# Batched fp32 matmul, A times B transposed: stores of batches 4 and 5 in parts in place of batch 11's

## The chip, the cores and the metric

The kernel runs on one core of a Trainium2 chip. The metric is the device time of one execution in microseconds, as the median of several runs. A profile of one execution goes with it; its span runs from the first to the last instruction.

## What is computed

For 16 batches the product of a 512 x 512 matrix with the transpose of another, in fp32:

```python
batch, m, k, n = 16, 512, 512, 512
np.matmul(a, b.transpose(0, 2, 1)).astype(np.float32)
```

Both inputs are 16.8 MB, and so is the output: 33.56 MB are read from HBM and 16.78 MB written.

## The kernel before

The 16 batches are worked off in 8 pairs `u`; a pair is batches `2u` (`e` = 0) and `2u+1` (`e` = 1).

**Loads.** A load brings the `a` or the `b` of one pair: 2 MB, on 128 partitions with 16 KB each. Load `n` is `a` of pair `n/2` for even `n`, `b` for odd `n`; there are 16. Seven buffers `ld` take them in turn (slot `n % 7`). Load 1 is issued by SP, all others by ACT: loads 0 to 6 at the start, then two at a time after the `ta` copies of a pair (lines 192 to 194).

**GpSimd** waits for each load in order and then adds one to `s_go` (lines 107, 108). DVE takes one of `s_go` before it reads a load.

**DVE** casts a load to bf16 in halves of K: the first half into `ha` or `hb`, the second into `wa` or `wb`, from where it is copied to `ha` or `hb` later.

**TensorE** transposes the bf16 blocks into PSUM (`tp`). ACT copies the transposed `a` into `ta` (line 181), DVE the transposed `b` into `tb` (line 168). Then come 32 matmuls of a pair (line 242), which write four PSUM banks `ps` for each batch.

**ACT** evicts `ps` into `ob` (line 201), four copies a batch. There are seven output buffers `ob`, so before it evicts batch `n` it waits until the store of batch `n - 7` has landed (line 198): `landed(n)` is semaphore `s_st[n % 7]` at a multiple of 16. ACT's instructions are in one fixed order for all pairs: eight `ta` copies, loads, four evictions of the first batch, four of the second. After the second batch's first and last eviction it adds one to `s_out`, so `s_out` at `n + 1` says that batch `n` is out of PSUM.

**Stores.** SP waits at the start for a second use of load slot 0 (line 120, load 7), then for `s_out` at `n + 1`, and stores batch `n`: 1 MB, each partition four consecutive rows of 2 KB, 8 KB in one run. The last batch is stored in two parts, the fourth row of each partition at the end (line 263).

**Batch 11 is stored otherwise** (`X = 11`). Its middle rows 1 and 2 of each partition go out as one DMA. Rows 0 and 3 go out in parts: SP stores partitions 32 to 95 in one DMA, then partitions 0 to 15 as four DMAs of four partitions each, then 16 to 19. GpSimd, after its loop over the loads, waits for `s_out` at 12 and issues four groups of three DMAs: a read of five short rows of `a` into `turn`, which nothing uses, then three partitions of 20 to 31, then eight of 96 to 127. SP's parts count on `s_x`, GpSimd's on `s_y`, and ACT waits for both at the end (lines 257, 258), together with the landings of the last seven stores.

Of the kernel before, what the change touches and what calls it, by code (L numbers as in the profile page):

```python
# [10 lines left out]
def kernel(  # L11
# [6 lines left out]
    nc = tc.nc  # L18
    P = 128
    batch, M, K = a.shape  # L20
    _, N, _ = b.shape
    J = M // P
# [3 lines left out]
    pairs = batch // 2  # L26
    f32 = mybir.dt.float32
    bf16 = mybir.dt.bfloat16
    NL = 7
    NO = 7  # L30
    X = 11

    def sbuf(name, shape, dtype):
        return ctx.enter_context(nc.sbuf_tensor(name, shape, dtype))

    def sem(name):
        return tc.alloc_semaphore(name)

    with tc.tile_critical(no_gpsimd_drain=True):  # L41
# [8 lines left out]
        ob = sbuf("ob", [P, NO, J, N], f32)  # L50
# [5 lines left out]
        s_ld = [sem(f"s_ld{i}") for i in range(NL)]  # L56
        s_st = [sem(f"s_st{i}") for i in range(NO)]

        s_go = sem("s_go")
# [11 lines left out]
        s_out = sem("s_out")  # L71
        s_x = sem("s_x")
        s_y = sem("s_y")
# [5 lines left out]
            out=ident[:], in_=ident[:], compare_op=mybir.AluOpType.not_equal, fill=1.0,  # L79
# [6 lines left out]
        def load(n, engine):  # L86
            u, slot = n // 2, n % NL
            src = (a if n % 2 == 0 else b)[2 * u:2 * u + 2].rearrange(
                "e (p j) k -> (e p) j k", j=2 * J
            )  # L90
            engine.dma_start(ld[:, slot], src).then_inc(s_ld[slot], 16)

        def landed(n):
            return s_st[n % NO], 16 * (n // NO + 1)

        def store(n, lo=0, hi=J, step=1, part=slice(0, P), engine=nc.sync):
            rows = slice(lo, hi, step)
            return engine.dma_start(  # L98
                out[n].rearrange("(p j) n -> p j n", j=J)[part, rows], ob[part, n % NO, rows]
            )  # L100

        load(0, nc.scalar)
# [1 line left out]
        for n in range(2, NL):  # L104
            load(n, nc.scalar)

        for n in range(2 * pairs):
            nc.gpsimd.wait_ge(s_ld[n % NL], 16 * (n // NL + 1)).then_inc(s_go, 1)  # L108

        nc.gpsimd.wait_ge(s_out, X + 1)
        for i in range(4):
            nc.gpsimd.dma_start(  # L114
                turn[:5, i], a[0, :5, :64].rearrange("p (x k) -> p x k", x=2)[:, :, :16]
            ).then_inc(s_y, 16)
            for part in (slice(20 + i, 32, 4), slice(96 + i, P, 4)):
                store(X, step=J - 1, part=part, engine=nc.gpsimd).then_inc(s_y, 16)

        nc.sync.wait_ge(s_ld[0], 32)  # L120
        for n in range(batch):
            nc.sync.wait_ge(s_out, n + 1)
            if n != X:
                store(n, hi=J if n < batch - 1 else J - 1).then_inc(landed(n)[0], 16)
                continue


            store(n, lo=1, hi=J - 1).then_inc(landed(n)[0], 16)
            store(n, step=J - 1, part=slice(32, 96)).then_inc(s_x, 16)
            for i in range(4):  # L130
                store(n, step=J - 1, part=slice(i, 16, 4)).then_inc(s_x, 16)
            store(n, step=J - 1, part=slice(16, 20)).then_inc(s_x, 16)

        def taker(engine):
            return lambda s, n: engine.wait_ge(s, n).then_inc(s, -n)  # L135
# [9 lines left out]
        with nc.Fori(0, pairs, engines=[dve]) as u:  # L145
            for x, (h, w, s_c, s_w) in enumerate(
# [4 lines left out]
                if x == 0:  # L151
# [4 lines left out]
                    out=h[:, J:, :], in_=src[:, J:, :HK]  # L156
                ).then_inc(s_c, 1)
                nc.vector.tensor_copy(out=w[:], in_=src[:, :, HK:]).then_inc(s_w, 1)  # L158
            for ko in range(KO):
# [5 lines left out]
                if ko == 1:  # L165
# [3 lines left out]
                    out=tb[:, ko, :],  # L169
# [7 lines left out]
        for u in range(pairs):  # L177
            for ko in range(KO):
                nc.scalar.wait_ge(s_ta, KO * u + ko + 1)
                for e in range(2):  # L180
                    c = nc.scalar.copy(  # L181
                        out=ta[:, ko, e * J * P:(e + 1) * J * P].rearrange(
                            "k (j p h) -> k j p h", j=J, h=2
                        ),
                        in_=tp[:, ko % 2, :, e * HP:(e + 1) * HP].rearrange(
                            "k (h j) p -> k j p h", h=2
                        ),
                    )
                c.then_inc(s_ea, 1)


            for n in (2 * u + NL, 2 * u + NL + 1):
                if n < 2 * pairs:
                    load(n, nc.scalar)
            for e in range(2):
                n = 2 * u + e
                if n >= NO:
                    nc.scalar.wait_ge(*landed(n - NO))
                for j in range(J):
                    nc.scalar.wait_ge(s_mm, J * n + j + 1)  # L200
                    c = nc.scalar.copy(  # L201
                        out=ob[:, n % NO, j, :].rearrange("m (p j) -> m p j", j=2 * J),
                        in_=ps[:, j, :].rearrange("m (j p) -> m p j", j=2 * J),
                    )
                    if e == 0:
                        c.then_inc(s_pv, 1)
                    elif j in (0, J - 1):
                        c.then_inc(s_out, 1)
# [45 lines left out]


    with tc.tile_critical(sync_engine=act, no_gpsimd_drain=True):
        nc.scalar.wait_ge(s_x, 16 * 6)
        nc.scalar.wait_ge(s_y, 16 * 12)
        for n in range(batch - NO, batch):
            nc.scalar.wait_ge(*landed(n))  # L260
    waits = nc.cur_bb.bb.instructions[-1]
# [38 lines left out]
```

## Time and profile before

| | before |
|---|---|
| median of 3 runs | 124.81 us (124.76 to 124.86) |
| profiled execution | 125.12 us |
| its span | 123.3 us |
| moved by DMA | 50.35 MB, mean 408 GB/s over the span |
| busy: PE, DVE, ACT, GpSimd | 73%, 55%, 55%, 7% of the span |
| store queue q1, load queue q10, GpSimd's q0 | 36.2%, 60.5%, 0.5% of 16 DMA engines' span |
| longest wait of ACT behind a store | 4.4 us, of 5.9 us in two |

The busy row of the page cuts the span into 40 slices of 3.1 us and gives each engine's busy share in tenths. The DMA row is the mean over the core's 16 DMA engines. "q10" holds the loads that ACT issues, "q1" what SP issues: load 1 and the stores. "q0" holds what GpSimd issues. A packet is one contiguous piece that one DMA engine moves. At the end of each DMA every engine that took part writes the semaphore, which the trace records as a packet of 4 bytes (a completion packet). In a timeline, the square brackets behind a group give the idle time before it and what ended it.

### The profile page before, as it was taken

The numbers are of one execution on the slowest core, as the hardware profiler recorded it, in microseconds if no ns is written. First come the engines' busy times: TensorE is split into PE (matmuls) and PEld (weight loads), VectorE is DVE, ScalarE is ACT, GpSimd is POOL, SyncE is SP. The second block draws the span as 40 slices with busy tenths as digits, with TensorE's granted clock in tenths as the row PEclk, the third lists the DMA queues.
The fourth block names the chain that finished last, engine by engine and source line by source line (L and its number), as shares of the span: only waits on it lengthen the run. The fifth ranks groups of instructions, "written<-read, shape, count | busy, mean of one in ns | idle before, by whom it ended". The sixth has DMA issues, their size and how long they took to land. (4 is left out here: it accounts for less than half of the span.)

```text
span 123.3 us, 2255 instructions
## 1 busy us (share of the span) xinstructions
PE 90.2 (73%) x768; PEld 54.8 (44%) x768; DVE 67.9 (55%) x96; ACT 67.9 (55%) x130; POOL 8.5 (7%) x18
## 2 busy tenths in 40 slices
PE   0000089999999899989998999999799917996000
PEld 0000078447744764574477347645654506542000
DVE  0000598982896589388918974872977059400000
ACT  0400064567855966696589468765866069656000
POOL 2000000000000000000000000000000039910000
PEclk9999999999999999999999999999999999999965
DMA  4999999999999999999999999999999999999991
GB/s 112 404 425 425 441 431 431 431 431 441 425 436 425 425 361 415 444 423 425 431 433 425 431 423 425 436 444 428 423 423 441 412 423 423 432 397 432 425 407 72
DMA packets 5341, 50.35 MB, mean 408 GB/s; under 512 B 904, under 2 KB 904, under 8 KB 1500
## 3 DMA queue, kind: packets, MB, share of 16 engines
q10 hardware_dynamic: 2160, 31.46, 60.5%
q1 hardware_dynamic: 2796, 18.70, 36.2%
q0 software_dynamic: 384, 0.18, 0.5%
q14 instruction: 1, 0.01, 0.0%
HBM read 33.56 MB, written 16.78 MB: 408 GB/s over the span
## 5 line engine op out<-in xcount | busy, mean ns | idle before, releaser
L242 PE MATMUL ps<-tb,ta 128*128 128x512 bf16 x256 | 57.8, 379 | 0.4
L201 ACT COPY ob<-ps 128x512 f32<-128x512 f32 x64 | 34.2, 591 | 27.8 <-PE ps L242 21.9
L181 ACT COPY ta<-tp 128x512 bf16<-128x512 bf16 x64 | 33.0, 612 | 13.7 <-PE tp L223 13.2
L242 PEld LDWEIGHTS ps<-tb,ta 128*128 128x128 bf16 x256 | 24.1, 98 | 30.6 <-issue 4.0
L223 PE MATMUL tp<-ident,ha 128*128 128x128 bf16 x256 | 18.6, 224 | 18.7 <-PEq L135 18.2
L223 PEld LDWEIGHTS tp<-ident,ha 128*128 128x128 bf16 x256 | 15.8, 100 | 22.3 <-issue 20.5
L168 DVE COPY tb<-tp 128x1024 bf16<-128x1024 bf16 x32 | 21.2, 685 | 3.6 <-DVEq L135 3.6
L223 PE MATMUL tp<-ident,hb 128*128 128x128 bf16 x256 | 17.6, 223 | 3.5 <-PEq L135 3.3
L223 PEld LDWEIGHTS tp<-ident,hb 128*128 128x128 bf16 x256 | 15.4, 100 | 4.7 <-issue 4.4
L154 DVE CAST ha<-ld 128x1024 bf16 x8 | 5.5, 690 | 14.6 <-POOLq L108 13.8
L163 DVE COPY ha<-wa 128x2048 bf16<-128x2048 bf16 x8 | 5.5, 691 | 12.7 <-DVEq L135 12.7
L154 DVE CAST hb<-ld 128x1024 bf16 x8 | 5.5, 689 | 7.9 <-DVEq L135 7.9
L158 DVE CAST wa<-ld 128x2048 bf16 x8 | 9.8, 1220 | 0.0
L158 DVE CAST wb<-ld 128x2048 bf16 x8 | 9.8, 1220 | 0.0
L114 POOL DMA_DIRECT2D turn<-in_a_dram x4 | 2.7, 663 | 98.9 <-ACT ob L201 98.9
L155 DVE CAST ha<-ld 128x1024 bf16 x8 | 5.5, 687 | 0.0
L155 DVE CAST hb<-ld 128x1024 bf16 x8 | 5.5, 686 | 0.0
L167 DVE COPY hb<-wb 128x2048 bf16<-128x2048 bf16 x8 | 5.5, 684 | 0.0
L98 POOL DMA_DIRECT2D out_dram<-ob x8 | 5.2, 651 | 0.0
L176 ACT ACT_TABLE_LOAD x1 | 1.3, 1283 | 4.1 <-issue 4.1
L78 POOL TENSOR_SCALAR_AFFINE_SELECT ident<-ident 128x128 bf16<-128x128 bf16 x1 | 0.3, 288 | 0.2 <-POOL ident L76 0.2
L76 POOL MEMSET ident<- 128x128 bf16 x1 | 0.2, 205 | 0.5 <-SPq L41 0.5
(5 smaller groups left out, 0.6 us busy)
## 6 DMA issues: line engine op xcount, KB each, us to landing
ld<-in_a_dram ACTq DMA_DIRECT2D x8, 2048.0 KB, 29.1
ld<-in_b_dram ACTq DMA_DIRECT2D x7, 2048.0 KB, 26.8
out_dram<-ob SPq DMA_DIRECT2D x14, 1024.0 KB, 29.0
ld<-in_b_dram SPq DMA_DIRECT2D x1, 2048.0 KB, 12.5
out_dram<-ob SPq DMA_DIRECT2D x1, 768.0 KB, 8.0
out_dram<-ob SPq DMA_DIRECT2D x1, 512.0 KB, 24.5
out_dram<-ob SPq DMA_DIRECT2D x2, 256.0 KB, 7.9
out_dram<-ob POOLq DMA_DIRECT2D x4, 32.0 KB, 6.0
```

Of the source, the lines that this page charges most:

```text
L98: return engine.dma_start(out[n].rearrange("(p j) n -> p j n", j=J)[part, rows], ob[part, n % NO, rows])
L114: nc.gpsimd.dma_start(turn[:5, i], a[0, :5, :64].rearrange("p (x k) -> p x k", x=2)[:, :, :16]).then_inc(s_y, 16)
L154: nc.vector.tensor_copy(out=h[:, :J, :], in_=src[:, :J, :HK])
L155: nc.vector.tensor_copy(out=h[:, J:, :], in_=src[:, J:, :HK]).then_inc(s_c, 1)
L158: nc.vector.tensor_copy(out=w[:], in_=src[:, :, HK:]).then_inc(s_w, 1)
L163: nc.vector.tensor_copy(out=ha[:], in_=wa[:]).then_inc(s_ca, 1)
L167: nc.vector.tensor_copy(out=hb[:], in_=wb[:]).then_inc(s_cb, 1)
L168: nc.vector.tensor_copy(out=tb[:, ko, :], in_=tp[:, 2 + ko % 2].rearrange("k j p -> k (j p)"),).then_inc(s_eb, 1)
L181: c = nc.scalar.copy(out=ta[:, ko, e * J * P:(e + 1) * J * P].rearrange("k (j p h) -> k j p h", j=J, h=2), in_=tp[:, ko % 2, :, e * HP:(e ...
L201: c = nc.scalar.copy(out=ob[:, n % NO, j, :].rearrange("m (p j) -> m p j", j=2 * J), in_=ps[:, j, :].rearrange("m (j p) -> m p j", j=2 * J),)
L223: t = nc.tensor.transpose(tp[:, 2 * x + g, j, :], h[:, j, g * P:(g + 1) * P], ident[:])
L242: t = nc.tensor.matmul(ps[:, j, :], ta[:, ko, (e * J + j) * P:(e * J + j + 1) * P], tb[:, ko, :].rearrange("k (j p) -> k j p", j=2 * J)[:, ...
```

## The change

The treatment in parts goes from batch 11, rows 0 and 3, to batches 4 and 5, rows 0 and 1 (`X = 4`, `H = 2`):

- Batches 4 and 5: SP stores rows 2 and 3 of each partition at the usual place, one DMA a batch, in runs of 4 KB. Directly after batch 5's, SP issues six DMAs, each over both batches: partitions 32 to 95, then five of four partitions each (0, 5, 10, 15; 1, 6, 11, 16; and so on to 4, 9, 14, 19).
- GpSimd's groups of three DMAs cover the same partitions as before, for both batches at once, in runs of 4 KB. They stand inside its loop over the loads: two groups after load 9, two after load 10, each time after a wait for `s_out` at 6.
- ACT's waits for `s_x` and `s_y` move from the end of the program to the place before batch 11's eviction (batch 11 reuses the buffer of batch 4, slot 4).
- Batch 11 is stored whole, like the others.

```diff
-    X = 11
+    X = 4
+    H = J // 2
@@
-        def store(n, lo=0, hi=J, step=1, part=slice(0, P), engine=nc.sync):
-            rows = slice(lo, hi, step)
+        def store(n, lo=0, hi=J):
+            return nc.sync.dma_start(
+                out[n].rearrange("(p j) n -> p j n", j=J)[:, lo:hi], ob[:, n % NO, lo:hi]
+            )
+
+        def store_two(part, engine):
+
             return engine.dma_start(
-                out[n].rearrange("(p j) n -> p j n", j=J)[part, rows], ob[part, n % NO, rows]
+                out[X:X + 2].rearrange("e (p j) n -> p e j n", j=J)[part, :, :H],
+                ob[part, X % NO:X % NO + 2, :H],
             )
@@
-        for n in range(2 * pairs):
-            nc.gpsimd.wait_ge(s_ld[n % NL], 16 * (n // NL + 1)).then_inc(s_go, 1)
-
-
-
-        nc.gpsimd.wait_ge(s_out, X + 1)
-        for i in range(4):
+        def spare(i):
             nc.gpsimd.dma_start(
                 turn[:5, i], a[0, :5, :64].rearrange("p (x k) -> p x k", x=2)[:, :, :16]
             ).then_inc(s_y, 16)
             for part in (slice(20 + i, 32, 4), slice(96 + i, P, 4)):
-                store(X, step=J - 1, part=part, engine=nc.gpsimd).then_inc(s_y, 16)
+                store_two(part, nc.gpsimd).then_inc(s_y, 16)
+
+        for n in range(2 * pairs):
+            nc.gpsimd.wait_ge(s_ld[n % NL], 16 * (n // NL + 1)).then_inc(s_go, 1)
+            if n in (X + 5, X + 6):
+                nc.gpsimd.wait_ge(s_out, X + 2)
+                for i in range(2):
+                    spare(2 * (n - X - 5) + i)
@@
-            if n != X:
-                store(n, hi=J if n < batch - 1 else J - 1).then_inc(landed(n)[0], 16)
-                continue
-
-
-            store(n, lo=1, hi=J - 1).then_inc(landed(n)[0], 16)
-            store(n, step=J - 1, part=slice(32, 96)).then_inc(s_x, 16)
-            for i in range(4):
-                store(n, step=J - 1, part=slice(i, 16, 4)).then_inc(s_x, 16)
-            store(n, step=J - 1, part=slice(16, 20)).then_inc(s_x, 16)
+            store(n, H if n in (X, X + 1) else 0, J if n < batch - 1 else J - 1).then_inc(
+                landed(n)[0], 16
+            )
+            if n == X + 1:
+
+
+                for part in (slice(32, 96), *(slice(i, i + 16, 5) for i in range(5))):
+                    store_two(part, nc.sync).then_inc(s_x, 16)
@@
                 if n >= NO:
                     nc.scalar.wait_ge(*landed(n - NO))
+                if n == X + NO:
+                    nc.scalar.wait_ge(s_x, 16 * 6)
+                    nc.scalar.wait_ge(s_y, 16 * 12)
@@
     with tc.tile_critical(sync_engine=act, no_gpsimd_drain=True):
-        nc.scalar.wait_ge(s_x, 16 * 6)
-        nc.scalar.wait_ge(s_y, 16 * 12)
         for n in range(batch - NO, batch):
             nc.scalar.wait_ge(*landed(n))
```

## The prediction

> **What bounds the kernel now.** I read the page first, for which resource is never idle. The engines' rows have gaps everywhere; the DMA row has none.
>
> ```profile
> PE   0000089999999899989998999999799917996000
> DMA  4999999999999999999999999999999999999991
> ```
>
> Then the table of stretches for the end, to see whether the transfers are still full once the last compute is over (columns: stretch, its length, PE, PEld, DVE, ACT, POOL, clock, DMA share, GB/s).
>
> ```profile
> 112.00:114.00 2.00, 0.83 (x4) 0.20 (x2) 0.00 (x0) 1.07 (x2) 0.00 (x0) 1.00 1.02 420
> ...
> 116.00:118.00 2.00, 0.00 (x0) 0.00 (x0) 0.00 (x0) 0.00 (x0) 0.00 (x0) 1.00 1.04 441
> 118.00:120.00 2.00, 0.00 (x0) 0.00 (x0) 0.00 (x0) 0.00 (x0) 0.00 (x0) 0.53 0.97 405
> ```
>
> Compute ends at 113.5 us and the DMA engines run full for eight more: 50.35 MB at full rate set the end. The chain of waits, which shows only PE and ACT and ends at 113.5, would mislead. The compute has slack, but little: the last two DMAs are issued at 113.5 and 114.3, and at 113.5 the store queue holds about 4.4 us of data ahead of them (the packet records show batch 15's packets from 117.95). Anything that delays ACT's last eviction by more than that, less about 1.5 us from issue to data, starves the DMA.
>
> Next, how the two big queues share the engines (page of the queues for 46 to 76 us; packets, MB, share of 16 engines).
>
> ```profile
> q10 hardware_dynamic: 586, 8.55, 67.0%
> q1 hardware_dynamic: 575, 4.21, 33.2%
> ```
>
> q10 is the loads (16 KB packets), q1 the stores (8 KB). 8.55 MB are 522 packets, 4.21 MB are 514: one for one, not byte for byte. From the shares (16 engines x 30 us = 480 engine-us), 0.670 x 480 / 522 = 0.616 us for a load packet, 0.332 x 480 / 514 = 0.310 us for a store packet. The packet records give the same: 611, 309, 159 and 84 ns for 16, 8, 4 and 2 KB, the next starting some 4 ns before the end; a pair takes 0.914 us, a store (8 packets an engine) 7.3 us. So the last completion packets of stores 3 to 6 are at 76.77, 84.19, 91.74 and 99.15 us, and the last load lands at 99.42.
>
> Last, ACT's timeline, where those landings come back to compute, through the seven output buffers:
>
> ```profile
> 84.91 2.05 ACT L201 COPY ob<-ps 128x512 f32<-128x512 f32 x4 [1.50 <-DMA out_dram<-ob]
> ...
> 99.84 2.05 ACT L201 COPY ob<-ps 128x512 f32<-128x512 f32 x4 [4.42 <-DMA out_dram<-ob]
> ```
>
> Batch 11 waits for store 4, batch 13 for store 6, each going on 0.7 us after the landing. These are the only stalls behind stores, and the change edits the first.
>
> **What the Trainium skill says.** "DMA: Bandwidth & Descriptors", section "Queues, rings and completion order": each DMA engine goes round its queues packet by packet. The 522 to 514 agrees. Same page, "Why a DMA increments its semaphore by 16 and not by 1": a DMA uses the largest number of engines up to 16 that divides the outer dimension, from SP the lowest-numbered. A four-partition DMA then runs on engines 0 to 3; the trace doesn't name engines, but q1's count of packets (2796) is right for 64 partitions on 16 engines and five such DMAs on four. "TensorE: Matmul & The Clock Gate", Part 1: an idle PE falls to half clock, and some 3.4 us of work bring it back. Here the clock was half at 118.1, 5.2 us after the last matmul, and full at 19.1, 3.8 us after the first; the cold start shows in PE's timeline:
>
> ```profile
> 15.36 1.87 PE L223 MATMUL tp<-ident,ha 128*128 128x128 bf16 x16 [15.36 <-PEq L135]
> ...
> 28.68 1.06 PE L223 MATMUL tp<-ident,ha 128*128 128x128 bf16 x16
> ```
>
> **The change, part by part.**
>
> Bytes. Engine 4 was spared 4 partitions x 2 rows of 2 KB: 8 x 0.080 = 0.64 us. Now it is 4 partitions x 2 batches of 4 KB: 8 x 0.155 = 1.24 us. Engines 0 to 3 carry two extra packets, 0.31 us for 0.16. By the last store's completion packets, one engine ends at 121.72, the next at 121.15, the rest between 120.5 and 121.1. If the last is engine 4, up to 0.57 us can be won; if not, nothing, or 0.15 lost on engines 0 to 3. Taken: -0.3 us, and only if the transfers still set the end.
>
> GpSimd. The twelve DMAs now stand inside the loop that passes each landed load to DVE through s_go: six after load 9, six after load 10. The new wait for s_out at 6 costs nothing: the value is there at 52.5, load 9 lands at 55.5. Behind them are s_go of loads 10 and 11, for which DVE waits. The four groups took 2.7, 1.76, 1.68 and 1.70 us. From 55.5 the first six end at about 60.0, before load 10 lands (62.8); the next six run from 62.8 to some 66.3, before load 11 (70.2). Hidden; with no cover they would delay a cast by up to 4.5 us.
>
> SP. Store 4 and store 5 become halves of 8 packets of 4 KB an engine. Then come, ahead of store 6, the 64-partition DMA (4 partitions x 2 batches, 8 packets) and five DMAs on engines 0 to 3 (10 packets). SP issues them at about 53 us, with 9 us to the next issue; the small ones cost it 0.6 to 0.75 us each, as at 87 to 90 us, so this is free. In q1, engines 0 to 3 now hold 34 packets of 4 KB where 16 of 8 KB stood, the others 24. This is the core of it: as the queues take turns by packet, each of these waits for one 16 KB load packet as long as loads remain. A turn moves half as much store data.
>
> ACT. The waits for s_x and s_y leave the end, where they cost nothing, and stand before batch 11's eviction. Before, it waited for store 4. Now it waits for everything down to the last small DMA behind stores 4 and 5. Behind the waiting instruction are batch 11's evictions, all `ta` copies of pairs 6 and 7 and all later evictions; behind those PE, SP's stores from batch 10 on, and the end.
>
> When does s_x arrive? Store 3's completion packets come from 75.15 to 76.77, median 75.7; these loads and stores are unchanged on engines 0 to 3. At that point some 25 load packets an engine are left (loads 13, 14, 15, and one of load 12). A turn is now 0.608 + 0.155 = 0.763 us. 25 turns: 19.1 us. The loads are then done, and the last 9 small-DMA packets follow alone: 9 x 0.155 = 1.4. So 20.5 us after 75.7 to 76.8: 96.2 to 97.3. On engines 5 to 15, GpSimd's 8 packets of 4 KB cost 1.3 us earlier, and 24 turns take 18.3: 94.7 to 96.4. I take 96.7. The loads end about 4 us earlier than before, which is where the stores' turns go; this doesn't help, as ACT stands still.
>
> From there, each duration from the timeline: wake-up 0.7, batch 11's evictions 2.05: 99.5 (before: 86.96). Pair 6 at the undisturbed pace (29.5, 41.0, 52.45: 11.5 us a pair) plus a cold PE, which has been idle since about 88: 32 transposes of the second half took 2.1 us warm, at half clock some 3.6; partly beside ACT's copies, so +1.1 (bounds 0 and 2): 112.1. Pair 7: 11.5, so ACT ends at 123.6, not 113.5. The stall of 4.42 us before batch 13 vanishes inside this: store 6 lands by about 99.
>
> And the DMA: stores 6 to 9 fill it from 96.7 to about 106, batches 10 and 11 to 111, 12 and 13 (out of ACT at 110 and 112) to about 116. Batch 14 leaves ACT only at 121.4. So it idles some 5 us. After 123.6: about 1.5 us from issue to data (first load: 1.0; SP's first: 1.9), 8 x 0.230 for 6 KB packets and 8 x 0.080 for the last row, together 2.5: 127.6. The program ended 1.6 after its last completion packet: span 129.2, which is 5.9 over 123.3. The profiled execution took 125.12, 1.8 around its span, and lies 0.3 over the median 124.81; I add the 5.9 to the median: 130.7 us.
>
> **The rivals.**
>
> *The wait is hidden (the faster side).* If s_x arrives early enough, ACT's end plus 4.0 us stays under 121.2, the DMA-bound end less engine 4's gain. Counting back (pairs 6 and 7: 24.1 warm and cold, evictions 2.05, wake-up 0.7), s_x must land by about 90.4, or 91.5 with a warm PE. That needs small packets to get more than one turn in two, sharing by bytes: 34 packets of 4 KB (5.3 us) beside 272 KB of loads (10.3 us) would land at about 91.5. The 522 to 514 speaks against it. Time then 124.3.
>
> *A shorter stall.* Turns shared somewhere between: s_x at 93 to 95. Nothing in the queues' page shows it, but 4 KB packets beside 16 KB ones don't occur before. Each us earlier is one us less: 127 to 129.
>
> *The PE stays warm*, or resumes with its work already done ahead: 129.6. The idle stretch of over 10 us, against the 5.2 after which the clock fell, is against it.
>
> *The spread doesn't do what it says* (engine numbers differ): bytes alone move, 0.3 us either way, and the ACT stall remains; within the main range.
>
> **How the numbers follow.** Full stall, cold or warm: 0.74, range 128.5 to 132.3 (s_x 96.2 to 97.3, cold 0 to 2, issue 1.0 to 1.9, 0.3 for the bytes). Shorter stall: 0.15. Hidden: 0.11, of it 0.08 faster and 0.03 within 0.2%, which is about what a measurement here can tell from no change. Slower: 0.89. For 8 in 10 the range reaches down into the shorter stall: 127.0 to 132.5.
>
> **What would show it.** ACT idle some 13 us before L201 at about 97, released by a store's DMA; PE idle from 88 to 100 and its clock at half just after; q1 packets of 4 KB one for one with q10's between 76 and 94; the last load earlier than 99.4; the DMA row with a hole near 116 to 121. I am wrong if batch 11's evictions begin before 92, or if the DMA row stays full to the end.

## The result and the profile after

| | before | after |
|---|---|---|
| median, compared on one chip | 124.84 us (4 runs) | 131.47 us (4 runs) |
| ratio to before | | 1.052 (95%: 1.047 to 1.057) |
| profiled execution | 125.12 us | 131.52 us |
| its span | 123.3 us | 129.7 us |
| ACT begins batch 11's eviction | 84.91 us | 97.13 us |
| ACT's last eviction ends | 113.5 us | 123.9 us |

The busy rows of the page, now of the changed kernel, with the granted clock of PE (in tenths) between them:

```profile
PE   0000289998999899899989989991000999989900
PEclk9999999999999999999999999999655579999995
DMA  5999999999999999999999999999999999970293
```

The DMA row has a hole near its end (slices are 3.24 us, so it lies between 116 and 123), and PE has one from slice 28. The table of stretches shows what runs while the DMA is empty (columns as before: stretch, length, PE, PEld, DVE, ACT, POOL, clock, DMA share, GB/s):

```profile
114.00:116.00 2.00, 1.91 (x33) 1.73 (x31) 1.55 (x4) 1.90 (x5) 0.00 (x0) 1.00 1.03 430
116.00:118.00 2.00, 1.95 (x11) 0.74 (x9) 1.08 (x2) 0.84 (x3) 0.00 (x0) 1.00 0.01 4
118.00:120.00 2.00, 2.00 (x11) 0.88 (x9) 0.00 (x0) 1.40 (x4) 0.00 (x0) 1.00 0.00 0
120.00:122.00 2.00, 2.00 (x11) 0.90 (x10) 0.00 (x0) 1.29 (x3) 0.00 (x0) 1.00 0.00 0
122.00:124.00 2.00, 1.22 (x6) 0.37 (x4) 0.00 (x0) 1.30 (x3) 0.00 (x0) 1.00 0.79 328
```

PE and ACT work off the last pair at their usual pace and nothing is there to be stored: no packet starts between 116.33 and 122.59 us. Those 6.3 us are nearly all of the 6.4 us that the span grew by. The queues' page agrees (packets, MB, share of 16 engines):

```profile
q10 hardware_dynamic: 2160, 31.46, 57.4%
q1 hardware_dynamic: 2796, 18.52, 34.2%
q0 software_dynamic: 512, 0.36, 0.9%
```

Together 92.5% of 129.7 us are 120.0 us of work for an engine in the mean, where before 97.2% of 123.3 us were 119.8. The transfers took as long as before; only the idle time grew. ACT's timeline shows where it comes from:

```profile
82.54 1.07 ACT L213 COPY ob<-ps 128x512 f32<-128x512 f32 x2 [0.60 <-PE ps L254]
97.13 2.05 ACT L213 COPY ob<-ps 128x512 f32<-128x512 f32 x4 [13.52 <-DMA out_dram<-ob]
```

The stall before batch 11 was 1.50 us and is 13.52 us. The semaphore records say which of the waits it is: the last update of `s_x` is at 97.06, that of `s_y` at 86.06. And the queues, 79 to 91 us, first before, then after (packets, MB, share of 16 engines):

```profile
q10 hardware_dynamic: 229, 3.49, 68.0%
q1 hardware_dynamic: 229, 1.63, 32.2%
```

```profile
q10 hardware_dynamic: 278, 4.03, 78.5%
q1 hardware_dynamic: 278, 1.01, 20.5%
q0 software_dynamic: 141, 0.10, 2.6%
```

One for one in packets of the two large queues in both; but in megabytes the stores' share fell from 1.63 to 1.01, as each of their packets holds 4 KB and not 8. The loads took what the stores gave up (the last one landed at 97.2 us and not at 99.8), which helped nobody.

### The profile page after: what moved, and what is told of

It reads as the page before. It is cut to its first block, busy times and chain, and to the rows that moved or that the text cites. A ratio compares the mean times of both kernels' runs of the same rounds, so it can differ in the third digit from the quotient of the medians.

```text
span 129.7 us, 2255 instructions
## 1 busy us (share of the span) xinstructions
PE 92.5 (71%) x768; PEld 56.9 (44%) x768; DVE 68.1 (53%) x96; ACT 67.9 (52%) x130; POOL 8.9 (7%) x18
## 5 line engine op out<-in xcount | busy, mean ns | idle before, releaser
L254 PE MATMUL ps<-tb,ta 128*128 128x512 bf16 x256 | 58.6, 383 | 0.4
L235 PE MATMUL tp<-ident,ha 128*128 128x128 bf16 x256 | 19.9, 232 | 29.9 <-PEq L144 29.4
L235 PEld LDWEIGHTS tp<-ident,ha 128*128 128x128 bf16 x256 | 16.8, 104 | 33.7 <-issue 31.9
L235 PE MATMUL tp<-ident,hb 128*128 128x128 bf16 x256 | 18.6, 230 | 0.5 <-PEq L144 0.5
L235 PEld LDWEIGHTS tp<-ident,hb 128*128 128x128 bf16 x256 | 16.3, 103 | 1.1 <-issue 0.7
```

Source lines behind the costliest of these rows:

```text
L235: t = nc.tensor.transpose(tp[:, 2 * x + g, j, :], h[:, j, g * P:(g + 1) * P], ident[:])
L254: t = nc.tensor.matmul(ps[:, j, :], ta[:, ko, (e * J + j) * P:(e * J + j + 1) * P], tb[:, ko, :].rearrange("k (j p) -> k j p", j=2 * J)[:, ...
```

## The experiments

The theories: *the wait* (the loss is how late ACT may go on with batch 11, and it is late since stores of 4 KB get half as much data through in a turn) and *the transfers* (small packets, four engines, GpSimd's queue make the moving itself slow). All times are medians; the ratio is to the kernel before on the same chip. The diffs are excerpts: what is left out of one (waits, counts, allocations that follow from it) is told in the text beside it.

| run | what it is | ACT goes on with batch 11 | time, us | ratio (95%) |
|---|---|---|---|---|
| wait_store5 | before, one later wait | 92.05 | 125.87 | 1.0061 (1.0044 to 1.0078) |
| wait_store6 | before, a still later wait | 98.74 | 133.21 | 1.064 (1.060 to 1.068) |
| own_buffer | change, without the wait's effect | 84.44 | 124.70 | 0.9967 (0.9956 to 0.9977) |
| one_dma_4k | change, no engine spared, no GpSimd | 97.21 | 131.31 | 1.052 (1.048 to 1.055) |
| whole_rows | batch 4 alone, runs of 8 KB | 90.91 | 126.95 | 1.016 (1.014 to 1.018) |
| spare_5 | whole_rows, dealt otherwise | 89.65 | 127.01 | 1.017 (1.015 to 1.020) |
| plain | before without parts | 84.22 | 125.29 | 1.0021 (1.0008 to 1.0034) |
| late_pair | the change on batches 9 and 10 | 83.93 | 124.64 | 0.9962 (0.9952 to 0.9972) |
| late_pair_3rows | the same with three rows | 84.45 | 125.33 | 1.0017 (1.0006 to 1.0029) |
| late_one_run | before, parts as 8 KB runs | 84.18 | 126.98 | 1.015 (1.013 to 1.017) |

**The wait alone.** Into the kernel before, with none of the change's transfers:

```diff
                     nc.scalar.wait_ge(*landed(n - NO))
+                if n == 11:
+                    nc.scalar.wait_ge(*landed(5))
```

> The kernel before, and only ACT's place before batch 11 changed: it waits for store 5 too. Theory 'the wait' (the time lies in how late ACT may evict batch 11; from there to ACT's end 26.8 us as measured after, then 5.8 to the end of the span once the DMA has run dry): store 5 lands at 91.7, ACT goes on at 92.4, ends at 119.2, span 125.0, time 126.5, 1.7 over before. Theory 'the transfers' (small packets, few engines and GpSimd's queue cost the time): 124.8, no change.

And with `landed(6)`:

> The kernel before, and ACT waits for store 6 before batch 11. 'The wait': store 6 lands at 99.15, ACT goes on at 99.9, ends at 126.6, span 132.4, time 134, later than the changed kernel, with none of its transfers. 'The transfers': 124.8.

The DMA row of the page and the stall in ACT's timeline, of wait_store5 and then of wait_store6:

```profile
DMA  4999999999999999999999999999999999999493
```

```profile
92.05 2.05 ACT L203 COPY ob<-ps 128x512 f32<-128x512 f32 x4 [7.67 <-DMA out_dram<-ob]
```

```profile
DMA  4999999999999999999999999999999997680193
```

```profile
98.74 2.05 ACT L203 COPY ob<-ps 128x512 f32<-128x512 f32 x4 [15.29 <-DMA out_dram<-ob]
```

A late eviction of batch 11 alone makes the same hole. Both gave somewhat less than expected. In wait_store6 (133.21 for 134) store 6 landed a us earlier than in before; of wait_store5 the profiled execution took 126.47, as expected, but the median was 125.87. The spans of the profiled executions go with ACT's time: 92.05 gave 124.7, 97.13 (the change) 129.7, 98.74 gave 131.7. Above 92 each us of delay costs about a us; the first seven, from 84.9 to 92.05, cost 1.4 together in these two executions and 0.8 by the medians.

**The transfers alone.** The changed kernel with all its transfers; only rows 0 and 1 of batch 11 get a buffer of their own, so the wait can stand one batch later (left out: SP's DMA that stores this buffer, and ACT's wait for it at the end):

```diff
+        ob2 = sbuf("ob2", [P, H, N], f32)
@@
-                if n == X + NO:
+                if n == X + NO + 1:
                     nc.scalar.wait_ge(s_x, 16 * 6)
@@
-                        out=ob[:, n % NO, j, :].rearrange(
+                        out=(ob2[:, j, :] if n == X + NO and j < H else ob[:, n % NO, j, :]).rearrange(
```

> The changed kernel with all its transfers where they are; rows 0 and 1 of batch 11 go to a 4 KB buffer of their own (stored by a DMA of its own), so that the wait for the parts stands before batch 12. 'The wait': batch 11 goes on at about 84, the wait comes at about 92 and ends at 97.1; from there one eviction of 6 us and one pair of 11.5: ACT ends at 115 to 116, the DMA never runs dry or for under 1 us; time 124.3 to 125.5. 'The transfers': 131.

Its DMA row, and ACT's timeline at batches 11 and 12:

```profile
DMA  4999999999999999999999999999999999999993
```

```profile
84.44 1.07 ACT L219 COPY ob<-ps 128x512 f32<-128x512 f32 x2 [0.94 <-DMA out_dram<-ob]
...
97.29 2.06 ACT L219 COPY ob<-ps 128x512 f32<-128x512 f32 x4 [6.09 <-DMA out_dram<-ob]
```

The parts land as late as in the change (ACT goes on at 97.29), but pair 6's transposes and the first half of its matmuls lie ahead of the wait now, and the hole is gone. All 6.6 us are back, and 0.3% more: the transfers, without the early wait, come out as a small gain. This is the run that decides between the two theories.

**Why `s_x` is late: the runs' size.** The six SP parts and twelve GpSimd DMAs are replaced by one (left out: GpSimd's issues, which go, and ACT's wait, now for this DMA alone):

```diff
-                for part in (slice(32, 96), *(slice(i, i + 16, 5) for i in range(5))):
-                    store_two(part, nc.sync).then_inc(s_x, 16)
+                store_two(slice(0, P), nc.sync).then_inc(s_x, 16)
```

> The changed kernel, but rows 0 and 1 of batches 4 and 5 go out as one DMA over all 128 partitions from SP: no engine is spared, GpSimd issues nothing, the runs stay 4 KB. If turns by packet make the wait long: 25 turns of 0.763 and 7 packets of 0.155 us after store 3, s_x at 96 to 97, ACT goes on at 97.2, time 131 to 132, as the change. If the five small DMAs on four engines or GpSimd's queue make it long: s_x by about 92, time under 127.

```profile
97.21 2.05 ACT L200 COPY ob<-ps 128x512 f32<-128x512 f32 x4 [12.99 <-DMA out_dram<-ob]
```

The same stall and the same time, with no small DMA, no engine spared and nothing from GpSimd. Beside wait_store5 it is a clean pair: the same bytes of batches 4 and 5, from the same buffers, in the same place of the queue, and the last completion packet at 91.68 us in packets of 8 KB, at 96.67 in packets of 4 KB. The 79 to 91 us of one_dma_4k:

```profile
q10 hardware_dynamic: 284, 4.13, 80.4%
q1 hardware_dynamic: 279, 1.01, 20.6%
```

**A cut that avoids the small runs, and failed.** Only batch 4 in parts, a run of 8 KB for each partition (left out: batch 5 is stored whole, GpSimd's groups stand one load earlier, and ACT waits only for the parts before batch 11):

```diff
-                out[X:X + 2].rearrange("e (p j) n -> p e j n", j=J)[part, :, :H],
-                ob[part, X % NO:X % NO + 2, :H],
+                out[X].rearrange("(p j) n -> p j n", j=J)[part], ob[part, X % NO]
```

> The change with another cut: only batch 4 goes out in parts, over the same partitions, all four rows of each in one run of 8 KB (the same 32 KB are kept from engine 4); GpSimd's groups stand after loads 8 and 9; batch 5 is stored whole; ACT still waits for the parts before batch 11. By turns: engines 0 to 3 hold 9 packets of 8 KB for batch 4 instead of 34 of 4 KB for both, 9 x 0.914 = 8.2 us after store 3, s_x at 84 to 85, ACT goes on at about 85.5 (before: 84.9), no hole in the DMA row. Time 124.2 to 124.8. If parts on few engines among the loads are the trouble whatever their size: a stall of more than 5 us and over 126.

I missed here. ACT goes on at 90.91, not 85.5:

```profile
90.91 2.05 ACT L209 COPY ob<-ps 128x512 f32<-128x512 f32 x4 [7.37 <-DMA out_dram<-ob]
```

The last updates of `s_x` come in steps of about 1.5 us (86.47, 87.93, 89.46; 87.78, 89.30, 90.88). One small DMA on one of its engines is one 8 KB packet and one completion packet of 4 bytes. With a 16 KB load packet ahead of each, that is 0.608 + 0.306 + 0.608 = 1.52 us: the completion packet takes a turn of its own. The packet records show it. On one engine a packet starts 3 or 4 ns before the end of the one ahead, so the records can be put into 16 sequences, one for each engine. One of the sequences with SP's small DMAs reads: part of 8 KB at 86.30 us, load 86.60, 4 bytes 87.21, load 87.22, part 87.82. So five small DMAs cost 7.6 us among loads and not 4.6, which is 3.0 of the 5.4 us by which the forecast was short. The other 2.4 came earlier: store 3, ahead of the parts in the queue, landed at 79.80 and not at 77.44. GpSimd's pieces were dealt out otherwise than meant (below), and three of the four engines with SP's small DMAs carried eight of them, 8 x 0.306 = 2.4 us. In the change the completion packets' turns are hidden, since there the parts outlast the loads (on these engines the loads end at 94.8 to 95.1 us, the parts at 96.4 to 96.7), and the sum of load and part packets is the same in any order.

The second miss is at the end: in whole_rows three engines wrote their last completion at 123.64 to 124.01 us, eleven at 121.8 to 122.0. The variant that was to spare engine 5 in place of engine 4 had the same trouble (its diff is against the change, and what is left out is as in whole_rows):

```diff
-                turn[:5, i], a[0, :5, :64].rearrange("p (x k) -> p x k", x=2)[:, :, :16]
+                turn[:6, i], a[0, :6, :64].rearrange("p (x k) -> p x k", x=2)[:, :, :16]
@@
-            for part in (slice(20 + i, 32, 4), slice(96 + i, P, 4)):
+            for part in (slice(24 + i, 32, 4), slice(96 + i, P, 4)):
@@
-                for part in (slice(32, 96), *(slice(i, i + 16, 5) for i in range(5))):
+                for part in (slice(32, 96), *(slice(i, 20, 4) for i in range(4)), slice(20, 24)):
```

> whole_rows with the partitions dealt out so that engine 5 and not engine 4 gets nothing (dummy read of 6 rows, GpSimd parts of two and eight partitions, SP parts of five and four). If it is engine 4 that ends last: 0.6 to 1.3 us slower than whole_rows. If sparing any engine, or only the place among the loads, brings the gain: the same as whole_rows.

It equals whole_rows within the intervals, but its time tells nothing of engine 4, as the engines end up to 4.1 us apart. To see this trouble without the wait, the kernel before with all four rows of batch 11 in its parts:

```diff
-                store(X, step=J - 1, part=part, engine=nc.gpsimd).then_inc(s_y, 16)
+                store(X, part=part, engine=nc.gpsimd).then_inc(s_y, 16)
```

(and likewise for SP's parts, without the DMA of rows 1 and 2).

> The kernel before, with all four rows of batch 11 in the parts: one run of 8 KB for each partition (32 KB kept from engine 4 on paper). If GpSimd's pieces fall on the engines as dealt whatever their dimensions: 124.4 to 124.8 and the last store's 16 completions within 1 us, as own_buffer. If its pieces with one run for each partition fall otherwise (as whole_rows and spare_5 suggest, whose completions lie 2 to 4 us apart): completions 3 to 4 us apart and 126 to 128.

```profile
DMA  4999999999999999999999999999999999999950
```

The DMA row drops early at its end, with no hole before: engines run out at different times. Eight write their last completion from 119.86 to 120.36 us, three from 120.83 to 121.39, two about 122.4, three from 123.48 to 123.86. That fits GpSimd's pieces of eight partitions lying on the eight lowest engines and those of three on the three lowest: engines 8 to 15 then lack four packets (1.2 us), engines 0 to 2 have nine too many (2.75 us). The Trainium skill, "DMA: Bandwidth & Descriptors", section "Why a DMA increments its semaphore by 16 and not by 1", names such an exception for some direct copies from GpSimd: a sixteenth of the partitions, rounded up, on each engine. The trace has no engine numbers, but the sequences put together as above show the same deal: eight with none of GpSimd's 8 KB pieces, five with four, three with eight. The two that end about 122.4 are the one that has both four such pieces and SP's small DMAs, and one with slow packets (told below). Where the pieces have two runs for each partition, the ends lie 0.85 us (own_buffer: 120.98 to 121.83) to 1.42 us (late_pair_3rows) apart, not 4.0.

**What the parts are worth without the wait.** The kernel before without any (left out: GpSimd's issues and the waits for the parts, which go too):

```diff
-            if n != X:
-                store(n, hi=J if n < batch - 1 else J - 1).then_inc(landed(n)[0], 16)
-                continue
+            store(n, hi=J if n < batch - 1 else J - 1).then_inc(landed(n)[0], 16)
```

> The kernel before without its parts: batch 11 stored whole like the others, GpSimd issues nothing. If engine 4 is the one that ends last, it gets 0.64 us of packets more and ends about 0.6 to 0.8 us later: 125.4 to 125.9. If another engine is the last, 124.8 to 125.0.

It is slower than before by 0.2% (0.35 us), which lies between the two expectations. Then the change on batches whose buffers are not used again, with the waits back at the end:

```diff
-    X = 4
+    X = 9
```

> The change moved to batches 9 and 10, whose buffers no later batch uses: the waits for the parts stand at the end of the program as before, GpSimd's groups after loads 14 and 15; cut, partitions and the 32 KB kept from engine 4 as in the change. If the wait before batch 11 is the whole loss and the bytes kept from engine 4 a small gain wherever they lie: no hole in the DMA row, ACT's stalls as before, 124.4 to 124.8, the same as own_buffer (0.9967). If only the place among the loads gains: 124.9 to 125.2.

> late_pair with three rows of each partition in the parts instead of two (runs of 6 KB): 48 KB kept from engine 4, 1.85 us of its packets, and 0.46 us more on engines 0 to 3. If engine 4 is still last with 32 KB kept away, faster than late_pair by 0.1 to 0.4; if engines 0 to 3 are last by then, slower by 0.1 to 0.3.

late_pair is the fastest of all runs, 0.38% under before; own_buffer is its equal within the intervals. So the gain goes with the 32 KB kept away, and the place among the loads is not needed. With 48 KB (`H = 3`) the gain is gone: 125.33, 0.7 us over late_pair, where at most 0.3 were expected. What sets the end there stays open. The DMA row of late_pair, and its only stall behind a store:

```profile
DMA  4999999999999999999999999999999999999993
```

```profile
ACT ob L210 <- DMA out_dram<-ob: 3.3, 1, 3.3
```

Which engine ends last can be read from the same sequences. In before the one that ends last (its last packet at 121.73 us, the next one's at 121.16) is the only one with neither pieces of GpSimd's nor SP's small DMAs: engine 4, though it carries the fewest bytes. Its 8 KB store packets take 318 ns in the mean, those of the others 309: 1.0 us in sum. Of the 63 such packets that took over 310 ns, 61 lie in this sequence. In plain one stands out in the same way (317 ns; 121.56 us, the next 120.83). In own_buffer it is again the one without parts (318 ns), and with 32 KB kept away it ends at 121.34, no longer last (121.50). A few records could belong to either of two sequences; these figures don't hang on them. Why this engine's store packets are slower no run shows.

## The prediction, step by step

**Right: the mechanism and its place.** The stall stands before batch 11, is released by `s_x`, comes from turns by packet, and starves the stores at the end. Its milestones: the last part's completion packet at 96.7 forecast, 96.72 measured; ACT on at 97.4, measured 97.13 (the forecast's 0.7 us from packet to ACT were 0.41: `s_x` had its last update at 97.06); pair 7 out at 123.6, measured 123.9; last completion packet at 127.6, measured 127.84; span 129.2, measured 129.7; median 130.7, measured 131.47.

**The term that was too small: the cold PE.** I added 1.1 us (bounds 0 and 2) to pair 6. PE's timeline after:

```profile
100.30 1.99 PE L235 MATMUL tp<-ident,ha 128*128 128x128 bf16 x16 [12.13 <-PEq L144]
102.09 1.91 PE L235 MATMUL tp<-ident,hb 128*128 128x128 bf16 x16
103.80 7.95 PE L254 MATMUL ps<-tb,ta 128*128 128x512 bf16 x32
```

Pair 6 took 13.24 us from the end of batch 11's eviction (99.18) to its own (112.42), where an undisturbed pair takes 11.47: 1.8 us. The clock was half from 91.9 to 105.6, so the restart lasted 5.3 us from the first transpose and not the 3.8 that I took from the start of before; the matmuls (7.95 for 7.29) were caught too. The 3.8 was one draw of many. In the twelve traces the first transpose of the program is 3.8 to 6.5 us ahead of the full clock (4.8 in the changed kernel itself), and after the stall it took 3.4 us in one_dma_4k and 6.0 in wait_store6. Pair 6 then took 12.4 and 13.6 us, 0.9 and 2.2 over an undisturbed one. The changes of clock lie on a raster: between two of them pass 71.68, 13.65 and 20.48 us in the changed kernel, 98.99 in before, which are 21, 4, 6 and 29 times 3.413. So where a restart falls in the raster is part of its cost, and a forecast from one trace can't know it: +1.1 was inside the spread, and that it came out at 1.8 is chance.

**Other terms.** From ACT's end to the last completion packet 3.95 us, forecast 4.0. From there to the end of the span 1.9, forecast 1.6. So the profiled execution lost 6.4 us where 5.9 were forecast: 0.6 more in pair 6 and 0.3 at the end, less 0.3 at ACT's restart. The medians lie 6.6 apart.

**GpSimd.** Its issues delayed no cast, as forecast: DVE begins its casts of loads 10, 11 and 12 at 68.70, 71.04 and 80.17 us, and began them at 68.50, 70.86 and 79.97, with the same 0.20 between the two executions as at load 8, before the first of these DMAs could matter. What I hadn't asked is when its transfers land: issued until 67.1 us, the last is counted in `s_y` at 86.06. By itself that would have held batch 11 up by some 1 us (84.91 before).

**Bytes.** The 0.3 us that I took for engine 4 don't show in the changed kernel, whose transfers no longer set the end. Where the wait is out of the way (own_buffer, late_pair) the gain is 0.36 to 0.52 us, and its condition, that the last engine is engine 4, holds by the sequences above.

**The rivals.** Sharing by bytes fell with the 278 to 278 packets. (Its sum set 136 KB of stores beside 272 KB of loads, which is the two to one of before; equal bytes would have come to 5.3 + 5.2 us, some 86 us.) For the hidden wait I had named 90.4 to 91.5 us as the latest `s_x`; wait_store5, whose store 5 had its last completion packet at 91.68, was 0.6% slower, so the threshold was about right. The shorter stall didn't occur, a PE that stays warm neither.

## What to carry to other kernels

When two queues are full and take turns by packet, as here, the length of the contiguous runs decides a queue's share: with runs of 4 KB and not 8 beside 16 KB loads the stores moved 1.01 MB and not 1.63 in 12 us, and every extra small DMA adds a completion packet that waits for a turn too. A wait that costs nothing at the end of a program is something else in the middle: before moving it, ask when the transfer lands in the new traffic, and how much compute is queued behind. To take work from one DMA engine, choose buffers that are not used again, and the wait can stay where it was (late_pair: 0.38% faster than before). A cold restart of PE is a range, not a number.

## What the runs showed that was not expected

- A completion packet takes a turn: small DMAs among loads completed 1.5 us apart, and 0.6 of it is the load packet ahead of the 4-byte one.
- GpSimd's small copies with one run for each partition left the engines up to 4.0 us apart at the end (119.86 to 123.86); with two runs each, 0.85 to 1.42 us.
- One engine's 8 KB store packets take 318 ns and not 309, and it ends last though it was given the fewest bytes (before).
- PE came back to full clock 3.4 to 6.0 us after its first transpose when it had been idle for 11.6 us or more, and 3.8 to 6.5 us after it at the start of the program; the changes lie whole multiples of 3.41 us apart.
